# The smallest block's threshold search at an earlier priority, and four query projections requested behind the branch section

## The chip, the cores and the metric

The kernel runs on one core of a Trainium2 chip. The metric is device time in microseconds (us) for one execution; the lower the better. The core has a matrix engine (TensorE, "PE" in the rows, with its weight loads as "PEld"), a vector engine (VectorE, "DVE"), a scalar engine (ScalarE, "ACT"), GpSimd ("POOL") and SyncE ("SP"), which issues most of the transfers. Each engine works through its own instructions in a fixed order; between engines they wait on semaphores.

## The reference

One decoder layer on 1024 tokens of width 1024. A combined projection feeds two mixers: a spatial gating unit, and a sparse attention in which a light indexer scores all keys and each query attends only to the best 256 of those that it may see. Output projection and a feed-forward part follow.

```python
h    = rms_norm(x, g_pre_mix) * (1 + sc1) + sh1
proj = einsum('bsd,de->bse', h, w_in)
p_u, p_v, p_q, p_k, p_val, p_qi, p_ki, p_wi = split_cols(proj)
y_a  = spatial_gating(gelu(p_u), gelu(p_v), ...)
y_b  = dsa_attention(q, k, v, q_idx, k_idx, p_wi)
o    = concat(rms_norm(y_a), rms_norm(y_b)) @ w_out
x    = x + g1 * rms_norm(o)
x    = x + g2 * rms_norm(relu(h2 @ w_ff1)**2 @ w_ff2)
...
# dsa_attention, per block of 128 queries:
score  = sum_h w_idx * relu(q_idx . k_idx)      # causal
_, idx = lax.top_k(score, 256)
logits = q . k[idx] ; o = softmax(logits) @ v[idx]
```

## The kernel before

Queries are worked on in eight blocks of 128. Block b sees 128*(b+1) keys, so blocks 0 and 1 need no selection (at most 256 keys) and blocks 2 to 7 do. Block 2 is the smallest of these, with 384 keys. In the rows the state tiles of a block's search are called `self_...`; where a row keeps its number, `self_2640` belongs to block 2, `self_2642` to block 3 and `self_2644` to block 4.

`select(b)` looks for the 256th best score by halving: 15 rounds, one for each bit of a 16-bit key. In `search` (blocks 7, 5 and 2) a round is three DVE instructions that depend on each other: a count over all keys (L603), a comparison (L605) and a step of the threshold (L607). In `search_signs` (blocks 6, 4 and 3, the tuple `ON_ACT`) the count is done by ACT (L615), and DVE does two small instructions (L616, L617) that wait for it. After a search come a few closing instructions (L637 to L646).

Instructions are placed on each engine by a scheduler that takes them by priority, a lower number first, when by its own clock they can run. The table `PRI` gives each `select(b)` its priority. At 465000 stands `search_rest`: it sums over all six blocks how many of them need a further search (`more`, L650), a PE instruction of size 1x1 (L652) adds it over the partitions, and `V.tensor_copy` (L653) puts it in `rest`. Then a branch section, kept together by `tile_critical`, loads `rest` into a register and jumps over the further search when it is zero. Behind it `mask(7)` (L671 to L686) makes the mask for block 7, with which attention goes on.

Attention is worked in the order `OB` = 0, 7, 1, 6, 5, 4, 3, 2. The query projections of the first four of `OB` (`q_proj`, 24 PE matmuls on L301, L303 and L304 each) are placed ahead; the other four are requested inside `search_rest` and are made to follow the flag matmul L652 on PE. Attention of block 0 needs no threshold, so PE and DVE do it before the branch section.

Of the kernel before, what the change touches and what calls it, by code (L numbers as in the profile page):

```python
# [37 lines left out]
def trunk(ctx, tc, x, c, positions, w_ada, b_ada, g_pre_mix, w_in, g_sgu_v, w_spatial, b_spatial,  # L38
# [8 lines left out]
    def nm(s):  # L47
        uid[0] += 1
        return f"{s}_{uid[0]}"
# [13 lines left out]
    def p_mm():  # L63
        return ps.tile([P, 512], F32, tag="mm", name=nm("mm"))

    def p_tr():
        return ps.tile([P, 512], F32, tag="tr", name=nm("tr"), bufs=3)
# [4 lines left out]
    def ct(shape, dt, name):  # L72
        return cst.tile(shape, dt, tag=name, name=name)
# [5 lines left out]
    def stage(n):  # L79
        tc.cur_priority = n * 100000  # L80

    def after(ins, prev):
        if prev is not None:
            tc.add_manual_dep(ins.ins, prev.ins.name,
                              mybir.DependencyInfo(mybir.DependencyClass.NoSync, mybir.DependencyReason.DATA),
                              reason="in this order")
# [209 lines left out]
    def proj(p, j, wt, n, ks=range(KD)):  # L296
        h, t = hT[j // 4], (j % 4) * P
        first = None
        for k in ks:
            lh, ll = h[:, 0, k, t:t + P], h[:, 1, k, t:t + P]  # L300
            mm = T.matmul(p[:, :n], lh, wt[k][:, 0, :n], start=k == 0, stop=False)  # L301
            first = first or mm
            T.matmul(p[:, :n], lh, wt[k][:, 1, :n], start=False, stop=False)  # L303
            T.matmul(p[:, :n], ll, wt[k][:, 0, :n], start=False, stop=k == KD - 1)  # L304
        return first

    def rope(t, j, nh, pool):

        q = t.rearrange("p (h e) -> p h e", h=nh)[:, :, 0:16]
        a = pool.tile([P, 8, 16], F32, tag="ropea", name=nm("ra"), bufs=1)[:, :nh]  # L310
        b = pool.tile([P, 8, 16], F32, tag="ropeb", name=nm("rb"), bufs=1)[:, :nh]
        cb = CS[:, 0, j, None, :].to_broadcast([P, nh, 16])
        sb = CS[:, 1, j, None, :].to_broadcast([P, nh, 16])
        G.tensor_tensor(a, q, cb, op=OP.mult)
        G.tensor_tensor(b, q, sb, op=OP.mult)
        G.tensor_tensor(q[:, :, 0:8], a[:, :, 0:8], b[:, :, 8:16], op=OP.subtract)
        G.tensor_tensor(q[:, :, 8:16], a[:, :, 8:16], b[:, :, 0:8], op=OP.add)
# [240 lines left out]
    OB = (0, 7, 1, 6, 5, 4, 3, 2)  # L558

    def q_proj(b, behind=None):  # L560
        p = p_mm()
        after(proj(p, b, wQ, 512), behind)
        QT[b] = qp.tile([P, 512], F32, tag="q", name=nm("q"), bufs=8)
        A.activation(QT[b], p, AF.Copy)
        rope(QT[b], b, 8, qp)
# [7 lines left out]


    stage(5)
    PRI = ((7, 400000), (6, 405000), (5, 415000), (4, 445000), (3, 455000), (2, 460000))
    nth = ct([P, 8], F32, "nth")
    for k in range(8):
        G.memset(nth[:, k:k + 1], float(k + 1))
# [18 lines left out]
    def search(u, top, tf, cnt, kd, kk, step=lambda: None):  # L598

        V.memset(tf, float(1 << top))  # L600
        for k in range(top, -1, -1):
            step()
            V.tensor_scalar(spare[:, :u.shape[-1]], u, tf, None, op0=OP.is_ge, op1=OP.add, accum_out=cnt)  # L603
            step()
            V.tensor_scalar(kk, cnt, kd, float(1 << k), op0=OP.is_ge, op1=OP.mult)  # L605
            step()
            V.scalar_tensor_tensor(tf, tf, -float(1 << (k - 1) if k else 1), kk, op0=OP.add, op1=OP.add)  # L607
# [40 lines left out]
    def search_rest():  # L648

        V.tensor_scalar(more[:, :6], KDS, 8.0, None, op0=OP.is_gt, op1=OP.add, accum_out=more[:, 6:7])  # L650
        p = p_tr()
        flag = T.matmul(p[:1, :1], more[:, 6:7], ones, start=True, stop=True)  # L652
        V.tensor_copy(rest, p[:1, :1])  # L653
        for b in OB[4:]:
            q_proj(b, flag)
        with tc.tile_critical():
            r = V.value_load(rest)
            with V.If(r > 0):
                for b in range(2, NB):
                    cnt, sg, kk, tf, kq, lf, top8, kd, th, lo, hi = ST[b]  # L660
                    search(BI[:, boff[b]:boff[b] + P * (b + 1)].bitcast(U16), 15, lf, cnt, kd, kk, V.drain)
                V.drain()

    masked, lowest = [None], [None]

# [21 lines left out]

    for b, pri in PRI:
        tc.cur_priority = pri
# [141 lines left out]
    for u, (b, grp, pair) in enumerate(units):  # L831
        if u == 3:
            at = tc.cur_priority
            tc.cur_priority = 465000
            search_rest()
            mask(7)
            tc.cur_priority = at
        if u + 1 < len(units):
            logits(u + 1)
        values(u)  # L840
        if u in MASKS:
            mask(MASKS[u])
        if u == 12:
            u_stack.close()
            sc_stack.close()
            o_stack, op_ = push("op")
        stack_for(u + 3)
        if u % 4 == 2:
            finish_a(b)
        if u in (24, 28):  # L850
            ada_use(u // 4 - 4)
        if u in (20, 24, 28):
            ADA[u // 4 - 3] = ada_sum(u // 4 - 3)
        if u % 4 == 0 and u:
            finish(OB[u // 4 - 1])
        if u == 14:
            WO[0] = w_chunk(w_out, [(0, 0, 512)], gout, tile_of=wo_tile)
        if u >= 19 and u % 2:
            oproj0(OB[(u - 19) // 2])
# [434 lines left out]
```

## Time and profile before

| | |
|---|---|
| median of 3 runs (lowest to highest) | 1246.16 us (1245.63 to 1246.74) |
| the profiled execution's own time | 1248.28 us |
| its span in the trace | 1246.4 us |
| PE, DVE, ACT, POOL busy (share of the span) | 1164.5 (93%), 873.8 (70%), 671.2 (54%), 209.4 us (17%) |
| mean granted TensorE clock | 0.967 of full speed |

The span is the trace's time from the first to the last instruction; 1.9 us of the profiled execution's time lie around it. Busy shares are averages over all stages, and matmuls that are in flight count as busy, so PE's share does not say that PE is the bound at each place.

### The profile page before, as it was taken

Reading aid. Unit: us, or ns where it says so; the run is one execution under the profiler, and the core shown is the slowest. Engines: PE = TensorE matmul, PEld = TensorE weight load, DVE = VectorE, ACT = ScalarE, POOL = GpSimd, SP = SyncE. Lnnn points to the kernel's source line nnn. Section 1 sums busy time; section 2 is a strip of 40 time slices with the busy share of each in tenths; the row PEclk is TensorE's granted clock in tenths of the full one; section 3 lists DMA queues with packets and bytes.
Section 4 is the critical chain, followed back from the end, with each engine's and each line's share of the span. In section 5 each row is a group of like instructions: output and inputs, shape, how many; then the busy total and the mean of one; then the engine's idle time right before and its main releaser. Section 6 shows DMA issues by size and latency. Waiting matters only on the chain.

```text
span 1246.4 us, 16883 instructions
## 1 busy us (share of the span) xinstructions
PE 1164.5 (93%) x5785; PEld 985.0 (79%) x5785; DVE 873.8 (70%) x1798; ACT 671.2 (54%) x1410; POOL 209.4 (17%) x304
## 2 busy tenths in 40 slices
PE   4899989995898999899899999999999999999997
PEld 4887768884697999887687788888887888888886
DVE  7844998968478666627898775655558756876568
ACT  4554679773266755537735455555544454445452
POOL 3585605451100000012610000000000000000001
PEclk9899989996898999999999999999999999999999
DMA  9431102110000144446315753544458455533335
GB/s 343 150 93 35 52 1 64 52 64 9 1 10 29 57 161 161 172 149 215 115 60 195 269 178 127 169 143 145 161 217 331 125 188 179 197 91 99 102 98 205
DMA packets 80239, 162.41 MB, mean 130 GB/s; under 512 B 7724, under 2 KB 32920, under 8 KB 80152
## 3 DMA queue, kind: packets, MB, share of 16 engines
q1 hardware_dynamic: 80136, 161.33, 38.3%
q8 instruction: 45, 0.74, 0.3%
q14 instruction: 42, 0.34, 0.1%
q10 hardware_dynamic: 16, 0.00, 0.0%
HBM read 119.36 MB, written 41.94 MB: 129 GB/s over the span
## 4 chain that ended last, share of the span: by engine, by line
PE 51%; DVE 12%; issue 4%; DMA 3%; ACT 2%; POOL 1%; SPq 0%; DVEq 0%; POOLq 0%; ACTq 0%
PE tr L1174 8%; PE lg L1174 8%; PE mm L1174 5%; PE mm L755 4%; PE lg L991 2%; PE lg L993 2%; PE lg L992 2%; PE tr L769 2%; PE lg L730 2%; PE tr L991 2%; PE tr L993 2%; PE tr L992 2%; DVE w L882 2%; PE mm L991 1%; PE mm L993 1%
## 5 line engine op out<-in xcount | busy, mean ns | idle before, releaser
L881 ACT ACTIVATE w<-rx 128x512 fp32r<-128x512 f32 x112 | 70.7, 632 | 148.1 <-PE lg L1174 64.5
L1174 PE MATMUL tr<-w,w 128*128 128x512 f32 x504 | 134.3, 392 | 2.9 <-DVE w L882 2.9
L1174 PE MATMUL lg<-w,w 128*128 128x512 f32 x504 | 133.7, 390 | 0.0
L882 DVE TENSOR_TENSOR w<-rx,w 128x512 fp32r<-128x512 f32 x112 | 77.2, 689 | 57.8 <-ACT w L881 57.1
L301 PE MATMUL mm<-w,hT 128*128 128x512 f32 (+1 forms) x288 | 112.8, 393 | 4.7 <-ACT hT L293 3.5
L1174 PEld LDWEIGHTS tr<-w,w 128*128 128x128 f32 x504 | 95.4, 189 | 23.2 <-DVE w L882 3.4
L303 PE MATMUL mm<-w,hT 128*128 128x512 f32 (+1 forms) x288 | 111.2, 387 | 0.0
L304 PE MATMUL mm<-w,hT 128*128 128x512 f32 (+1 forms) x288 | 110.2, 384 | 1.0 <-POOL hT L294 1.0
L1174 PEld LDWEIGHTS lg<-w,w 128*128 128x128 f32 x504 | 94.9, 188 | 19.7
L1210 POOL TENSOR_TENSOR rsf<-rsf,mhalf 128x1 f32<-128x1 f32 x8 | 6.0, 752 | 605.6 <-DVE rsf L1209 605.6
L1174 PE MATMUL mm<-w,w 128*128 128x512 f32 x336 | 93.9, 389 | 0.0
L755 PEld LDWEIGHTS mm<-VV,pT 128*128 128x128 f32 x576 | 76.1, 199 | 3.8 <-ACT pT L750 1.6
L755 PE MATMUL mm<-VV,pT 128*128 128x64 f32 x576 | 76.4, 277 | 0.9 <-ACT pT L750 0.9
L1174 PEld LDWEIGHTS mm<-w,w 128*128 128x128 f32 x336 | 63.1, 188 | 13.2
L882 DVE TENSOR_TENSOR w<-b,w 128x512 fp32r<-128x512 f32 x96 | 65.7, 685 | 4.0 <-ACT w L881 4.0
L301 PEld LDWEIGHTS mm<-w,hT 128*128 128x128 f32 x288 | 55.8, 194 | 14.9 <-ACT hT L293 3.7
L730 PE MATMUL lg<-KS,qs 128*128 128x512 f32 (+5 forms) x192 | 55.3, 399 | 10.6 <-DVE mxs L731 6.0
L882 DVE TENSOR_TENSOR w<-s,w 128x512 fp32r<-128x512 f32 x56 | 38.2, 688 | 37.3 <-ACT w L881 37.3
L304 PEld LDWEIGHTS mm<-w,hT 128*128 128x128 f32 x288 | 55.0, 191 | 10.5 <-POOL hT L294 1.3
L734 ACT ACTIVATE L<-L,mxs 128x128 f32<-128x128 f32 (+7 forms) x64 | 49.2, 771 | 25.8 <-DVE mxs L731 25.6
L881 ACT ACTIVATE w<-b 128x512 fp32r<-128x512 f32 x96 | 59.4, 618 | 6.7 <-DMA b<-in_w_ff_dram 6.5
L303 PEld LDWEIGHTS mm<-w,hT 128*128 128x128 f32 x288 | 55.5, 193 | 8.5
(356 smaller groups left out, 2975.5 us busy)
## 6 DMA issues: line engine op xcount, KB each, us to landing
rx<-x_scratch SPq DMA_DIRECT2D x56, 512.0 KB, 3.5
x_scratch<-d SPq DMA_DIRECT2D x108, 256.0 KB, 3.0
ada<-in_w_ada_dram SPq DMA_DIRECT2D x48, 512.0 KB, 5.6
raw<-in_w_ff_dram SPq DMA_DIRECT2D x32, 512.0 KB, 4.1
b<-in_w_ff_dram SPq DMA_DIRECT2D x32, 512.0 KB, 4.6
x<-in_x_dram SPq DMA_DIRECT2D x16, 512.0 KB, 5.6
raw<-in_w_in_dram SPq DMA_DIRECT2D x8, 512.0 KB, 3.6
raw<-in_w_in_dram SPq DMA_DIRECT2D x16, 256.0 KB, 2.8
```

Of the source, the lines that this page charges most:

```text
L301: mm = T.matmul(p[:, :n], lh, wt[k][:, 0, :n], start=k == 0, stop=False)
L303: T.matmul(p[:, :n], lh, wt[k][:, 1, :n], start=False, stop=False)
L304: T.matmul(p[:, :n], ll, wt[k][:, 0, :n], start=False, stop=k == KD - 1)
L730: T.matmul(pl, QS[b, grp][:, q, h4 * P:(h4 + 1) * P], KS[:, grp, c0:c0 + cw], start=q == 0, stop=q == 1)
L734: ex = A.activation(L, L, AF.Exp, scale=-1.0, bias=top, accum_out=sms[:, b, h:h + 1])
L755: mm = T.matmul(po[:, o:o + 64], e[:, (si * 2 + h2) * P:(si * 2 + h2 + 1) * P], VV[:, s0 + si, grp], start=first, stop=pair == 1 and s0 + ...
L881: A.activation(hi, src, AF.Copy)
L882: eng.tensor_tensor(lo, src, hi.bitcast(F32), op=OP.subtract)
L991: ms.append(T.matmul(p, a[:, 0, k], b[:, 0, k], start=start and k == 0, stop=False, skip_group_check=more))
L992: ms.append(T.matmul(p, a[:, 0, k], b[:, 1, k], start=False, stop=False, skip_group_check=more))
L993: ms.append(T.matmul(p, a[:, 1, k], b[:, 0, k], start=False, stop=stop and k == 3, skip_group_check=more))
L1174: ms.append(T.matmul(p, x[:, qa, t * P:(t + 1) * P], y[:, qb], start=start and n == 0, stop=stop and n == 2, skip_group_check=more))
```

## The change

Two edits. Block 2's `select` is moved in `PRI` from 460000 (behind block 3) to 445000 (the number of block 4, ahead of block 3's 455000). And the loop that requests the four late query projections stands in `search_rest` behind the branch section in place of ahead of it.

```diff
-    PRI = ((7, 400000), (6, 405000), (5, 415000), (4, 445000), (3, 455000), (2, 460000))
+    PRI = ((7, 400000), (6, 405000), (5, 415000), (4, 445000), (2, 445000), (3, 455000))
...
         V.tensor_copy(rest, p[:1, :1])
-        for b in OB[4:]:
-            q_proj(b, flag)
         with tc.tile_critical():
             r = V.value_load(rest)
             with V.If(r > 0):
                 for b in range(2, NB):
                     cnt, sg, kk, tf, kq, lf, top8, kd, th, lo, hi = ST[b]
                     search(BI[:, boff[b]:boff[b] + P * (b + 1)].bitcast(U16), 15, lf, cnt, kd, kk, V.drain)
                 V.drain()
+        for b in OB[4:]:
+            q_proj(b, flag)
```

On DVE, in the stretch where block 3 searches on ACT: rows of block 2's search (`self_2640`, 384 keys) now stand between those of block 3's (`self_2642`). `ya` belongs to the gating unit.

```order
+L605 TENSOR_SCALAR self_2640<-self_2640,kds 128x1
 L616 TENSOR_SCALAR self_2642<-self_2642 128x1
+L607 SCALAR_TENSOR_TENSOR self_2640<-self_2640 128x1
 L617 SCALAR_TENSOR_TENSOR self_2642<-self_2642 128x1
+L603 TENSOR_SCALAR spare,self_2640<-BI,self_2640 128x384
+L540 SCALAR_TENSOR_TENSOR ya_2553<-tr_2552,cols,uv_2436 128x128 x2
+L605 TENSOR_SCALAR self_2640<-self_2640,kds 128x1
 L616 TENSOR_SCALAR self_2642<-self_2642 128x1
+L607 SCALAR_TENSOR_TENSOR self_2640<-self_2640 128x1
 L617 SCALAR_TENSOR_TENSOR self_2642<-self_2642 128x1
```

All 15 rounds of block 2 now stand so, about one to each of block 3's rounds; before, they stood behind block 3's last round, among the rows of block 0's attention and after them.

On DVE ahead of the branch section, before (with the semaphores that an instruction waits for):

```order
L650 TENSOR_SCALAR more<-kds 128x6
L644 MAX self_2640<-BI 128x8 [waits DVE_49]
L653 CAST rest<-tr_3131 1x1 [waits PE_49]
L646 ISA pick,self_2640<-pick,self_2640 128x8 [waits DVE_49]
L646 ISA self_2640 128x1
L656 NO_OP [waits DVE_49,Activation_49,Pool_49]
L1290 UNCONDITIONAL_BRANCH [waits DMAHW2_49,DMAHW1_49,DMAHW3_49,DMAHW0_49,DMAHW4_49,DVE_sequencer_49,DMAHW5_49,DVE_49,DMAHW6_49,PE_49,DMAHW7_49,Activation_49,Pool_49]
```

And in the change:

```order
L779 RECIPROCAL sms<-sms 128x4 [waits Activation_49]
L780 TENSOR_TENSOR yb_3083<-mm_3056,sms 128x256 [waits DVE_49,PE_49]
L795 TENSOR_SCALAR ya_3116<-ya_3116,rsa 128x512 [waits DMAHW2_49,Pool_49]
L653 CAST rest<-tr_3131 1x1 [waits PE_49]
L654 NO_OP [waits DVE_49,Activation_49,Pool_49]
L1290 UNCONDITIONAL_BRANCH [waits DMAHW2_49,DMAHW1_49,DMAHW3_49,DMAHW0_49,DMAHW4_49,DVE_sequencer_49,DMAHW5_49,DVE_49,DMAHW6_49,PE_49,DMAHW7_49,Activation_49,Pool_49]
```

The sum `more` now stands ahead of block 0's attention on DVE, so the flag follows that attention directly; the branch waits for the same engines as before, PE among them.

On PE at the place where DVE's branch section begins, before (`mm_3134` is the first late query projection):

```order
L301 MATMUL mm_3134<-w_2472,hT_143 128x512
L303 MATMUL mm_3134<-w_2472,hT_143 128x512
L1290 UNCONDITIONAL_BRANCH
L304 MATMUL mm_3134<-w_2472,hT_143 128x512
L301 MATMUL mm_3134<-w_2475,hT_143 128x512
L303 MATMUL mm_3134<-w_2475,hT_143 128x512
L304 MATMUL mm_3134<-w_2475,hT_143 128x512
```

And in the change (the same projection is `mm_3725`):

```order
L301 MATMUL mm_3725<-w_2472,hT_143 128x512
L303 MATMUL mm_3725<-w_2472,hT_143 128x512
L1290 UNCONDITIONAL_BRANCH
L304 MATMUL mm_3725<-w_2472,hT_143 128x512
L301 MATMUL mm_3725<-w_2475,hT_143 128x512
L303 MATMUL mm_3725<-w_2475,hT_143 128x512
L304 MATMUL mm_3725<-w_2475,hT_143 128x512
L709 MATMUL tr_3123<-ident,ya_3116 128x128 x3
```

In both, 20 of the projection's 24 matmuls stand between L652 and this point. Three of the four transposes of block 0's `ya` (L709), which stood ahead of L652, now stand behind the projection; and the four transposes of the second query stack of block 0 (L322), which stood behind the first logits that read the stack's low part, now stand ahead of them. SP's order is the same.

## Rows read from the trace of the kernel before

**Rows 1.** The page's chain of work that ended last, by engine

```profile
PE 51%; DVE 12%; issue 4%; DMA 3%; ACT 2%; POOL 1%; SPq 0%; DVEq 0%; POOLq 0%; ACTq 0%
```

**Rows 2.** PE's waits, 283 to 346 us: total, times, longest

```profile
PE tr L652 <- DVE more L650: 9.5, 1, 9.5
PE lg L730 <- DVE mxs L731: 5.2, 1, 5.2
```

**Rows 3.** PE's timeline, 283 to 345: start, duration, instruction, idle before and releaser

```profile
288.54 0.90 PE L730 MATMUL lg<-KS,qs 128*128 128x128 f32 x3 [3.66 <-DVE qs L392]
289.24 1.07 PE L322 MATMUL tr<-ident,qd 128*128 128x128 f32 x4
...
299.63 1.00 PE L709 MATMUL tr<-ident,ya 128*128 128x128 f32 x4
310.12 0.19 PE L652 MATMUL tr<-ones,more 128*1 128x1 f32 x2 [9.48 <-DVE more L650]
...
316.47 0.39 PE L303 MATMUL mm<-w,hT 128*128 128x512 f32 x1
...
329.43 1.22 PE L730 MATMUL lg<-KS,qs 128*128 128x512 f32 x2 [5.24 <-DVE mxs L731]
```

**Rows 4.** DVE's timeline near 300 us: one round of block 2

```profile
299.56 0.61 DVE L603 TENSOR_SCALAR_CACHE_REDUCE spare<-BI,self 128x384 int8<-128x384 int16 x1
...
300.21 0.21 DVE L605 TENSOR_SCALAR self<-self,kds 128x1 f32<-128x1 f32 x1
300.46 0.16 DVE L607 SCALAR_TENSOR_TENSOR self<-self 128x1 f32<-128x1 f32 x1
```

**Rows 5.** Line L603, 285 to 309: count, ns min/median/max, first and last start

```profile
L603 DVE TENSOR_SCALAR_CACHE_REDUCE spare<-BI,self x15: 601/612/614, 285.6 to 307.3; 128x384 int8<-128x384 int16 x15
```

**Rows 6.** Timeline of all engines, 267 to 271: rounds of block 3

```profile
267.42 0.21 DVE L616 TENSOR_SCALAR self<-self 128x1 f32<-128x1 f32 x1 [0.71 <-ACT spare L615]
...
267.67 0.16 DVE L617 SCALAR_TENSOR_TENSOR self<-self 128x1 f32<-128x1 f32 x1
...
267.92 0.72 ACT L615 ACTIVATE spare<-BI,self 128x512 int8<-128x512 int16 x1 [0.53 <-DVE self L617]
...
268.77 0.21 DVE L616 TENSOR_SCALAR self<-self 128x1 f32<-128x1 f32 x1 [0.95 <-ACT spare L615]
...
270.46 0.61 DVE L540 SCALAR_TENSOR_TENSOR ya<-tr,cols,uv 128x128 f32<-128x128 f32 x2
```

**Rows 7.** DVE's timeline near 246: blocks 5 and 4 search side by side

```profile
246.00 1.01 DVE L603 TENSOR_SCALAR_CACHE_REDUCE spare<-BI,self 128x768 int8<-128x768 int16 x1
...
247.51 1.01 DVE L603 TENSOR_SCALAR_CACHE_REDUCE spare<-BI,self 128x768 int8<-128x768 int16 x1
```

**Rows 8.** Busy time by stretch: length, then each engine, clock, DMA

```profile
258.12:265.14 7.02, 7.02 (x35) 5.88 (x34) 6.64 (x21) 3.21 (x9) 6.42 (x7) 1.00 0.22 75
265.14:283.33 18.19, 18.02 (x86) 14.89 (x84) 7.25 (x36) 13.92 (x42) 7.90 (x19) 1.00 0.21 66
283.33:300.63 17.30, 12.77 (x55) 10.97 (x53) 14.81 (x65) 7.87 (x24) 3.45 (x8) 0.61 0.00 0
```

**Rows 9.** Timeline of all engines near 263

```profile
262.89 1.29 POOL L222 TENSOR_TENSOR w<-raw,w 128x512 fp32r<-128x512 f32 x1
...
263.34 0.85 DVE L617 SCALAR_TENSOR_TENSOR self<-self 128x1 f32<-128x1 f32 x1
```

**Rows 10.** Line L617, 265 to 283.5: count, ns min/median/max

```profile
L617 DVE SCALAR_TENSOR_TENSOR self<-self x13: 159/160/286, 265.4 to 283.0; 128x1 f32<-128x1 f32 x13
```

**Rows 11.** The branch's line, 300 to 330: DVE's queue waits, ns min/median/max

```profile
L1290 DVEq EVENT_SEMAPHORE  x6: 50/50/5610, 310.9 to 317.0; - x6
```

**Rows 12.** DVE's timeline around the branch section

```profile
310.36 0.13 DVE L653 CAST rest<-tr 1x1 int32<-1x1 f32 x1
...
321.01 0.15 DVE L671 CAST seli<-self 128x1 int32<-128x1 f32 x1 [10.36 <-DVEq L656]
```

**Rows 13.** PE's waits, 345 to 640, the largest: total, times, longest

```profile
PE tr L904 <- ACT x L947: 6.2, 1, 6.2
```

## The prediction

> **What bounds the kernel now.** I began with the chain of work that ended last: half of it is PE and an eighth DVE [rows 1], so a change on DVE is worth what PE waits for it. Next I read PE's own waits in the stretch that the two edits touch. There are two of size: 9.5 us until `more` (L650) is there, so that the flag matmul can run, and 5.2 us later for DVE's `mxs` [rows 2]. PE's timeline shows where they lie. PE begins block 0's attention proper at 288.54, ends it with the transposes of `ya` at 300.63 (299.63 + 1.00), stands still until L652 at 310.12, and after the query projections stands again until 329.43 [rows 3].
>
> DVE's rows name what PE waits for at 300 to 310: rounds of block 2's search, one after the other, each a chain of L603, L605, L607 [rows 4]. All 15 begin between 285.6 and 307.3 [rows 5], behind block 3's search. Yet while block 3 searched, DVE was mostly idle. A round of block 3 is 1.35 us long (267.42 to 268.77), ACT counts through most of it, and DVE waits 0.95 us of it [rows 6]; over 265.14 to 283.33 DVE is busy for 7.25 of 18.19 us [rows 8].
>
> The second wait is a sequel of the first. After the flag's copy at 310.36 DVE stands at the branch section until L671 at 321.01 [rows 12], 5.61 us of it in one semaphore wait that ends at 317.0 [rows 11]. That is just behind the end of the 20th matmul of the first late projection (316.47 + 0.39 = 316.86 [rows 3]), the last one ahead of the branch's place on PE. Then `mask(7)` runs, and only after it can PE go on. So everything from L652 to 329.43 hangs on L652 and should move with it.
>
> **Edit 1, block 2's priority.** No work is removed: 15 rounds of 0.61 + 0.21 + 0.16 = 0.98 us move from the exposed place into block 3's search. What it takes away is PE's 9.48 us for `more` [rows 3], because the rows of the change have `more` ahead of block 0's attention. What it costs is a later end of block 3's search, and with it a later start of that attention. I work this out in four pieces.
>
> - A plain round costs nothing. L603, its accumulator read and L605 occupy DVE from 299.56 to 300.42 (300.21 + 0.21) [rows 4], 0.86 us, and the gap is 0.95 [rows 6]. L607 fits between L616 and L617, which start 0.25 apart because the second waits for the first. If this cover were too small, the rounds would stretch. The nearest row from above is blocks 5 and 4 side by side: 1.51 us for a round with twice the keys (246.00 to 247.51) [rows 7]. At that rate 14 rounds would cost 14 x (1.51 - 1.35) = 2.2. I take 0, since 384 keys need 0.4 us less than 768 (0.61 against 1.01).
> - At the start, 258.12 to 265.14, there is no gap: DVE is busy 6.64 of 7.02 us [rows 8], with block 4's closing instructions. The change puts one whole round here. I take 1.0 (0.98, rounded); bounds 0 and two rounds, 2.0.
> - Two rounds also hold a `ya` pair of 0.61 us [rows 6]. 0.86 + 0.61 is 1.47 against 0.95, so at most 0.5 each. I take 0.6 for both; bounds 0 and 1.0.
> - POOL works more in this stretch than where the rounds stood: 6.42 of 7.02 and 7.90 of 18.19 us, against 3.45 of 17.30 [rows 8]. One L617 took 0.85 us under a POOL operation that ran from 262.89 to 264.18 [rows 9], where its median is 0.16 [rows 10]. I take one such hold, 0.7; bounds 0 and two, 1.4.
>
> The Trainium skill, page "SBUF — State Buffer", section "Who interferes with whom", says why: a DVE instruction with two SBUF inputs contends with a GpSimd instruction that reads SBUF, and the one that starts second is blocked until the other ends. By that rule L607 may be held wherever POOL reads. The trace agrees at 263.34 with 0.69 us, but only there.
>
> Together the start of block 0's attention is 2.3 us later, with bounds 0 and 2.2 + 2.0 + 1.0 + 1.4 = 6.6. The closing instructions of block 2 now come ahead of that attention too, but in their place two rounds of block 2 that stood there are gone; I set these equal.
>
> **The two small moves on PE.** Three of the four `ya` transposes leave the place ahead of L652: 0.75 of 1.00 us [rows 3]. Four query-stack transposes, 0.7 us from 289.24 to the next start, go ahead of 288.54, where PE is idle for 3.66 us anyway [rows 3]. That is 1.45 us less between the start of the attention and L652; if PE waits for DVE there rather than for itself, it is 0. What could be gained beyond it: DVE now answers block 0's logits with no search rounds in between. PE is dense in that stretch, at a granted clock of 0.61 [rows 8], so I count nothing. Should the clock be full there, about 10.6 us of work would shrink by 10.6 x 0.39 = 4.1; that is the bound on the other side.
>
> **Edit 2, the projections behind the branch section.** I cost it at nothing. The built order still has the same 20 matmuls between L652 and the branch's place, and DVE's branch still names PE among the engines that it waits for. SP's order is unchanged, so no transfer moves against another; the four late projections run in the same places and are still waited on by ACT's copies and POOL's rotary steps in the same order.
>
> **The sum.** L652 comes 9.48 + 1.45 - 2.3 = 8.6 us earlier, so does the branch, `mask(7)` (L671 at 312.4 in place of 321.01) and PE's resumption (320.8 in place of 329.43). Behind that the orders differ only in neighbouring rows, and PE's waits there, the largest 6.2 us for ACT [rows 13], are for work that hangs on the same chain and moves too. The profiled execution would take 1248.28 - 8.6 = 1239.7. The median of the runs lies 2.12 us below the profiled one, so 1246.16 - 8.6 = 1237.5 us.
>
> **The rivals.**
> - *Rounds add instead of overlapping* (slower). If a round of block 3 became as long as its own 1.35 plus block 2's 0.98, block 3 would end 14 x 0.98 = 13.7 us later in place of 2.3. Then 9.48 + 1.45 - 13.7 = -2.8, and 1249.0. It decides from 10.9 / 14 = 0.78 us per round. For it: the engine runs its instructions in order, and a late L605 delays L616. Against it: 1.51 us for blocks 5 and 4 together [rows 7], although their DVE part alone is longer than block 2's.
> - *POOL holds most of the moved steps.* If all 15 L607 were held for 0.69 us, 10.4 in place of 0.7, the gain would be 8.6 - 9.7 = -1.1, and 1247.3. Against it: of 13 L617 between 265 and 283.5 the longest took 0.286 us [rows 10]. The Trainium skill's rule above, carried to its end, is this case.
> - *The lead is lost later.* If some engine behind 329 us were already bound by something that does not move, PE would wait there instead: 1246.2. For it, PE has waits up to 6.2 us later on; against it, their releasers are ACT and DVE, not transfers [rows 13].
> - *Edit 2 does free the branch*, so that DVE no longer waits for the projection: 5.6 us more [rows 11], 1231.9. Against it: the order above. The rival that edit 2 does nothing is my forecast.
>
> **How the numbers follow.** The forecast has 0.80, the rounds that add 0.06, the holds 0.04, the lost lead 0.05, the freed branch 0.05. Gains run from 9.48 + 1.45 - 6.6 = 4.3 (1241.9) to 9.48 + 1.45 + 4.1 = 15.0 (1231.1) if every cost were nothing and the clock full; that corner needs two things together, so I stop at 1231.5, which takes in the freed branch. Range 1231.5 to 1242. Within 0.2% (2.5 us, about what a measurement of this kernel can tell from no change) fall the holds and the lost lead, 0.09; slower 0.06; faster 0.85.
>
> **What would show it.** Right: L652 without a wait for `more`; L603 rows of 384 keys from about 260 to 285, one to each L616; rounds of block 3 still near 1.35 us; block 0's attention beginning on PE near 290.8; the long semaphore wait at the branch still there, near 5 to 6 us. Wrong: rounds of 2 us or more, L607 of 0.5 us and over in numbers, a new wait of PE ahead of block 0's attention of more than 10 us, or a branch section that no longer waits.

## The result, and the profile after

The changed kernel takes 1232.14 us (median of 6 runs, 1230.24 to 1233.56); the kernel before, on the same chip, took 1246.05 us (6 runs, 1239.45 to 1246.74). The ratio is 0.9896, with a 95% interval from 0.9875 to 0.9918: 13.9 us faster. The forecast was 1237.5 us, so the sign and the range held, and the gain was 5.3 us larger than worked out. The profiled execution took 1231.81 us, its span 1229.8 us, and the mean granted clock was 0.977 (0.967 before).

The first lines of the page of the changed kernel (busy time by engine; the chain that ended last):

```profile
PE 1156.0 (94%) x5785; PEld 977.9 (80%) x5785; DVE 869.4 (71%) x1798; ACT 671.2 (55%) x1410; POOL 208.6 (17%) x304
...
PE 57%; DVE 10%; DMA 3%; issue 2%; ACT 2%; POOL 1%; SPq 0%; DVEq 0%; POOLq 0%; ACTq 0%
```

PE, DVE, ACT and POOL are busy for nearly as long as before; the chain has 57% of PE where it had 51% [rows 1]. PE's waits from 283 to 346 us in the changed kernel (total, times, longest):

```profile
PE lg L730 <- DVE mxs L731: 4.8, 1, 4.8
...
```

The 9.5 us for `more` [rows 2] are gone; the wait for `mxs` is still there, 0.4 us shorter. PE's timeline of the changed kernel:

```profile
289.69 1.83 PE L730 MATMUL lg<-KS,qs 128*128 128x128 f32 x6 [4.25 <-DVE qs L392]
...
298.37 0.19 PE L652 MATMUL tr<-ones,more 128*1 128x1 f32 x2
298.49 0.50 PE L301 MATMUL mm<-w,hT 128*128 128x512 f32 x1
...
315.88 3.10 PE L730 MATMUL lg<-KS,qs 128*128 128x512 f32 x6 [4.80 <-DVE mxs L731]
```

Block 0's attention begins at 289.69 (288.54 before, [rows 3]), L652 runs at 298.37 with nothing to wait for (310.12), and PE goes on behind `mask(7)` at 315.88 (329.43). All 15 rounds of block 2 now lie beside block 3's search. Lines L603 and L607 of the changed kernel, 258 to 290 (count, ns min/median/max, first and last start):

```profile
L603 DVE TENSOR_SCALAR_CACHE_REDUCE spare<-BI,self x15: 600/605/613, 260.4 to 283.8; 128x384 int8<-128x384 int16 x15
L607 DVE SCALAR_TENSOR_TENSOR self<-self x15: 146/149/434, 264.9 to 284.7; 128x1 f32<-128x1 f32 x15
```

And how a round of each fits into the other, in the timeline of all engines of the changed kernel:

```profile
268.87 0.21 DVE L616 TENSOR_SCALAR self<-self 128x1 f32<-128x1 f32 x1
...
269.20 0.60 DVE L603 TENSOR_SCALAR_CACHE_REDUCE spare<-BI,self 128x384 int8<-128x384 int16 x1
...
269.37 0.72 ACT L615 ACTIVATE spare<-BI,self 128x512 int8<-128x512 int16 x1
...
269.85 0.21 DVE L605 TENSOR_SCALAR self<-self,kds 128x1 f32<-128x1 f32 x1
...
270.22 0.21 DVE L616 TENSOR_SCALAR self<-self 128x1 f32<-128x1 f32 x1 [0.16 <-ACT spare L615]
```

This round of block 3 is still 1.35 us long (268.87 to 270.22), and DVE, after a whole round of block 2 inside it, still waits 0.16 us for ACT. By stretch (length, then PE, PEld, DVE, ACT and POOL busy, clock, DMA):

```profile
258.12:265.14 7.02, 7.02 (x35) 5.88 (x34) 6.99 (x21) 3.26 (x12) 6.80 (x10) 1.00 0.27 75
265.14:284.35 19.21, 17.77 (x84) 14.47 (x82) 17.49 (x95) 14.95 (x41) 7.53 (x19) 1.00 0.21 63
...
289.69:298.37 8.68, 8.65 (x42) 7.82 (x43) 4.99 (x26) 5.03 (x20) 0.61 (x1) 0.64 0.00 0
```

In the second stretch DVE was busy for 7.25 us before [rows 8] and for 17.49 us now; the stretch is 1.0 us longer. The last line is block 0's attention up to L652: 8.68 us, where it was 12.09 (288.54 to 300.63) [rows 3]. The branch's wait on DVE, and the first instruction behind it:

```profile
L1290 DVEq EVENT_SEMAPHORE  x6: 50/50/3985, 299.0 to 303.4; - x6
```
```profile
307.47 0.15 DVE L671 CAST seli<-self 128x1 int32<-128x1 f32 x1 [8.72 <-DVEq L654]
```

The wait is 3.99 us, 1.6 less than in [rows 11]. The clock that was granted to PE, in the changed kernel:

```profile
289.69:294.00 4.31, 4.28 (x20) 0.50 0.00 0
...
296.00:298.37 2.37, 2.37 (x15) 1.00 0.00 0
298.37:303.50 5.13, 5.13 (x25) 1.00 0.00 0
```

and in the kernel before:

```profile
288.54:298.50 9.96, 9.82 (x43) 0.50 0.00 0
298.50:300.63 2.13, 2.13 (x8) 0.54 0.02 4
...
310.12:314.00 3.88, 3.88 (x11) 0.50 0.00 0
314.00:317.00 3.00, 3.00 (x15) 0.98 0.00 0
```

Both kernels begin block 0's attention at the lower level (1.2 GHz). In the kernel before PE stays at it nearly to the end of that attention, stands still for 9.48 us and begins the late projection at it again; in the changed kernel PE is at 2.4 GHz from about 296 on.

### The profile page after: what moved, and what is told of

It is laid out like the page before. It is cut to its first block, busy times and chain, and to the rows that moved or that the text cites. A ratio compares the mean times of both kernels' runs of the same rounds, so it can differ in the third digit from the quotient of the medians.

```text
span 1229.8 us, 16884 instructions
## 1 busy us (share of the span) xinstructions
PE 1156.0 (94%) x5785; PEld 977.9 (80%) x5785; DVE 869.4 (71%) x1798; ACT 671.2 (55%) x1410; POOL 208.6 (17%) x304
## 4 chain that ended last, share of the span: by engine, by line
PE 57%; DVE 10%; DMA 3%; issue 2%; ACT 2%; POOL 1%; SPq 0%; DVEq 0%; POOLq 0%; ACTq 0%
PE tr L1174 8%; PE lg L1174 8%; PE mm L1174 6%; PE mm L755 4%; PE lg L991 3%; PE lg L993 3%; PE lg L992 3%; PE tr L991 2%; PE tr L993 2%; PE tr L992 2%; PE mm L993 2%; PE mm L992 2%; PE mm L991 2%; PE tr L769 2%; PE lg L730 2%
## 5 line engine op out<-in xcount | busy, mean ns | idle before, releaser
L304 PEld LDWEIGHTS mm<-w,hT 128*128 128x128 f32 x288 | 54.7, 190 | 10.2 <-POOL hT L294 1.0
L730 PE MATMUL lg<-KS,qs 128*128 128x512 f32 (+5 forms) x192 | 52.2, 384 | 10.7 <-DVE mxs L731 5.7
```

What stands on the lines that cost most here:

```text
L730: T.matmul(pl, QS[b, grp][:, q, h4 * P:(h4 + 1) * P], KS[:, grp, c0:c0 + cw], start=q == 0, stop=q == 1)
```

## The experiments

Starting times in different traces are compared as they stand. The traces of before and of the change are in step to 0.04 us ahead of block 2's rounds (L638 of block 4 at 259.02 and 259.06), but those of the other runs reach that place up to 1.6 us earlier or 0.6 later. Where that matters, the text counts from a nearer place.

The theory was that the moved search is nearly the whole gain, that edit 2 does nothing, and that the 5.3 us beyond the forecast come from a shorter stretch of block 0 and from the clock at the projection. Rivals were that edit 2 frees the branch, that the cover in block 3's search is not what made the move cheap, and that the shorter stretch comes from PE's clock or from DVE alone.

### Edit 1 alone

The kernel before with the new `PRI` line and nothing else.

```diff
-    PRI = ((7, 400000), (6, 405000), (5, 415000), (4, 445000), (3, 455000), (2, 460000))
+    PRI = ((7, 400000), (6, 405000), (5, 415000), (4, 445000), (2, 445000), (3, 455000))
```

> Edit 1 alone; the four projections stay requested ahead of the branch section. Theory (the whole gain is edit 1, edit 2 changes no engine's order): the changed kernel's time, 1232 us within 2, and a DVE wait at the branch of about 4 us as there. Rival (edit 2 frees part of the branch wait): slower than the changed kernel by 1.5 to 5 us.

Measured: 1232.89 us (1231.61 to 1236.97), ratio 0.991 [0.9885, 0.9935]. L652 runs at 298.38 and PE goes on at 315.96. Within the spread, edit 1 is the whole gain. One thing differs from the changed kernel: this execution begins block 0's attention 0.7 us earlier (288.98) and needs 9.40 us up to L652 in place of 8.68, with the same 42 matmuls in the same order. What that shows of the clock is taken up further down.

### Edit 2 alone

The kernel before with the second edit and nothing else.

```diff
-        for b in OB[4:]:
-            q_proj(b, flag)
         with tc.tile_critical():
...
                 V.drain()
+        for b in OB[4:]:
+            q_proj(b, flag)
```

> Edit 2 alone; block 2's search stays behind block 3's. Theory: no change from the kernel before, 1246 us within 2.5, with PE's 9.5 us wait for the sum and DVE's 5.6 us wait at the branch as there. Rival: 2 to 6 us faster, with a shorter wait at the branch.

Measured: 1244.51 us (1239.77 to 1248.03), ratio 0.9992 [0.9975, 1.001]: no change. PE's waits, 283 to 346, and DVE's branch line:

```profile
PE tr L652 <- DVE more L650: 9.9, 1, 9.9
PE lg L730 <- DVE mxs L731: 5.2, 1, 5.2
```
```profile
L1290 DVEq EVENT_SEMAPHORE  x6: 49/50/5250, 309.6 to 315.3; - x6
```

Both waits of PE are there as in the kernel before, and the branch's wait, 5.25 us, is near its 5.61. Requesting the projections behind the section does not move them behind it, as the built order showed.

### The branch truly freed

The changed kernel; the late projections follow the first DVE instruction of `mask(7)` in place of the flag matmul, so that all 24 matmuls of the first one stand behind the branch's place on PE (`opened[0]` is that first instruction).

```diff
-        for b in OB[4:]:
-            q_proj(b, flag)
...
             mask(7)
+            for b_ in OB[4:]:
+                q_proj(b_, opened[0])
```

> The changed kernel, but the projections are requested behind the mask of block 7 and made to follow its first DVE instruction in the scheduler's order, so that none of their matmuls stands ahead of the branch on PE; no wait between engines is added. Theory (DVE's wait at the branch is for the 20 matmuls of the first projection): that wait falls from 4.0 us to under 1, the mask of block 7 starts 3 to 4 us earlier, PE resumes 3 to 4 us earlier, and the time is 1228 to 1229.5 us. Rival (the section is held by its own load and fetch, or PE loses elsewhere what DVE gains): 1231 to 1233.

Measured: 1226.69 us (1221.6 to 1230.18), ratio 0.9861 [0.9836, 0.9885], a larger gain than the 1228 to 1229.5 us expected. It is the lowest median so far; its interval and that of edit 1 alone, from the same runs of before, only touch, at 0.9885, and it overlaps that of the changed kernel by 0.001. DVE's branch line, and PE's first logits behind `mask(7)`:

```profile
L1291 DVEq EVENT_SEMAPHORE  x6: 49/50/353, 298.1 to 298.9; - x6
```
```profile
322.31 1.53 PE L729 MATMUL lg<-KS,qs 128*128 128x512 f32 x6
```

The wait fell from 3.99 to 0.35 us, `mask(7)` begins at 302.92 in place of 307.47 (5.47 us behind the flag, and 9.10 in the changed kernel), and PE meets no wait for `mxs` there (4.80 us in the changed kernel). All 96 matmuls of the four late projections now stand ahead of those logits; in the changed kernel 48 do, and the logits behind the other 48 begin at 330.69.

### The idle stretch ahead of block 0's attention filled

The changed kernel with 18 matmuls added on PE (their result is not used) in the 4.25 us wait ahead of block 0's attention. For that the second query stack (`stack_for(2)`) is requested ahead of them in place of behind the first logits.

```diff
     stack_for(0)
+    at = tc.cur_priority
+    tc.cur_priority = 465000
+    stack_for(2)
+    tc.cur_priority = at
+    pf = p_mm()
+    for i in range(18):
+        T.matmul(pf, hT[0][:, 0, i % KD, :P], wQ[i % KD][:, 0], start=True, stop=True)
     logits(0)
-    stack_for(2)
```

> The changed kernel with 18 extra 128x512 matmuls (4.1 us at full clock) into an unused tile on PE, in the 4.3 us that it idles ahead of block 0's attention; their result is not read. Theory (the lower granted clock after that idle time costs time in block 0's attention, 289.7 to 298.4): the clock stays at full there, the stretch of 8.7 us shrinks by 1.5 to 3, and the time falls by as much, 1229 to 1231 us. Rival (the stretch is bound by the hand-overs between PE, DVE and ACT, so that the clock does not matter): 8.7 us still, and 1232 us or a little more for the extra work.

Measured: 1229.84 us (1225.79 to 1229.95), ratio 0.9865 [0.9839, 0.989]. PE's wait fell to 0.94 us, yet the granted clock of its stretches was:

```profile
288.35:290.00 1.65, 1.05 (x6) 1.00 0.00 0
290.00:292.00 2.00, 1.94 (x12) 0.75 0.00 0
292.00:294.00 2.00, 2.00 (x13) 0.50 0.00 0
```

The clock fell all the same, inside the stretch in place of ahead of it, and the stretch up to L652 took 8.40 us in place of 8.68. The time lies in the range that was expected for a clock that stays up, but not for that reason. From L618, the end of block 3's search, to L652 it is 13.54 us (283.21 to 296.75) where the changed kernel takes 14.02 (284.35 to 298.37): 0.5 us of the 2.3 by the medians. No row here accounts for the rest. So this run does not tell what a full clock all through would be worth.

### Block 2's count done twice

The changed kernel, in which each round of block 2 does its L603 a second time (added work, the same threshold).

```diff
             V.tensor_scalar(spare[:, :u.shape[-1]], u, tf, None, op0=OP.is_ge, op1=OP.add, accum_out=cnt)
+            if twice:
+                V.tensor_scalar(spare[:, :u.shape[-1]], u, tf, None, op0=OP.is_ge, op1=OP.add, accum_out=cnt)
...
-            search(u, 14, tf, cnt, kd, kk)
+            search(u, 14, tf, cnt, kd, kk, twice=b == 2)
```

> The changed kernel, but each of block 2's 15 rounds makes its count twice (0.6 us more on DVE per round; the second count gives the same number). Theory (a round is hidden because its 0.86 us fit in DVE's 0.95 us gap, and hardly more fits): rounds of block 3 stretch from 1.35 to about 1.9 us, block 3's search ends 7 to 8 us later, and the time is 1238 to 1241 us. Rival (DVE has room, the cover is much larger than a round): under 3 us later, 1232 to 1235.

Measured: 1242.34 us (1240.25 to 1249.0), ratio 0.9974 [0.9954, 0.9994]. One of block 3's rounds (L616 is L618 here) in DVE's timeline, from its start to the next:

```profile
273.15 0.21 DVE L618 TENSOR_SCALAR self<-self 128x1 f32<-128x1 f32 x1
275.09 0.21 DVE L618 TENSOR_SCALAR self<-self 128x1 f32<-128x1 f32 x1
```

The one shown takes 1.94 us in place of 1.35, and the twelve from 265.42 to 287.33 take 1.83 on average (1.34 to 2.27). PE waits 2.8 us for `more` again. So the gap of 0.95 us that ACT's count leaves on DVE is the cover, and a round that is larger than it does stretch block 3. The size was not met. Counted from L638 (L640 here, at 258.12), block 3's search ends 6.6 us later than in the changed kernel (7 to 8 expected), the flag runs 5.9 and `mask(7)` begins 7.5 us later, and 10.2 of the 13.9 us are lost, more than expected. What is lost behind `mask(7)` no row here shows.

### Block 0's attention with DVE loaded

The changed kernel with 8 counts over 384 keys (4.9 us of DVE's time in the trace) added on DVE among block 0's logits, where the kernel before had its search rounds; the counts go to a tile of their own.

```diff
+                if b == 0:
+                    V.tensor_scalar(spare[:, :384], BI[:, boff[2]:boff[3]].bitcast(I16), 0.0, None, op0=OP.is_ge,
+                                    op1=OP.add, accum_out=load)
```

> The changed kernel with eight extra counts of 384 keys (0.69 us each with their accumulator read, 5.5 us in all, result not read) on DVE among the logits of block 0's attention, where seven rounds of block 2 stood in the kernel before. Theory (that stretch became shorter mainly because PE's work is dense enough to get its full clock back by 294.9; a DVE that answers later thins PE's work and keeps the clock low): the stretch grows from 8.7 to 10.5 us or more, the clock is at half through most of it, and the first late projection starts at the half clock; 1234.5 to 1238 us. Rival (DVE's answers are hidden, PE's own work sets the stretch): 8.7 to 9.3 us, and 1232 to 1233 us.

Measured: 1234.4 us (1231.01 to 1235.63), ratio 0.990 [0.9878, 0.9922]. The granted clock of PE's stretches:

```profile
294.00:297.00 3.00, 2.97 (x15) 0.50 0.00 0
297.00:299.72 2.72, 2.72 (x15) 0.92 0.00 0
```

The stretch is 9.84 us long, 1.16 more than in the changed kernel and 2.25 less than before. It falls between the two expectations. All of the 1.16 us lies ahead of the first long logits (128x512): from the start to them it is 7.03 us (289.88 to 296.91) where the changed kernel takes 5.84 (289.69 to 295.53). So a loaded DVE can hold up this stretch in the new order. The last part, with the full clock, is there with or without the load (2.81 and 2.84 us).

### PE's wait for the flag filled, in part

The kernel before with 28 added matmuls ahead of the flag matmul, into a tile that the flag overwrites.

```diff
         p = p_tr()
+        for i in range(28):
+            T.matmul(p, hT[0][:, 0, i % KD, :P], wQ[i % KD][:, 0], start=True, stop=True)
         flag = T.matmul(p[:1, :1], more[:, 6:7], ones, start=True, stop=True)
```

> The kernel before, with 28 added 128x512 matmuls on PE between the transposes of block 0's ya and the flag matmul, into a tile that the flag matmul overwrites afterwards, so that PE works through most of its 9.48 us wait for more. Nothing else is moved but the last transposes and values of block 0, which now stand ahead of the flag. The clock theory (about 1.7 us of the change's gain is the first late projection at the full clock, because PE no longer stands still ahead of it): the granted clock at the projection is 1.00 in place of 0.50, DVE's long wait at the branch falls from 5.6 to about 4.0 us, mask(7) begins 1.6 us earlier behind the flag, and the time falls by 1 to 2 us, 1244 to 1245. The rival (the branch wait fell for another reason, such as what stands ahead of it on DVE, and the projection's clock does not matter): the wait stays at 5.3 us or more and the time is that of the kernel before, within 1 us. If the fill itself runs past DVE's last round, the flag is late, and L652 will show a wait for nothing but PE.

Measured: 1246.51 us (1242.94 to 1249.45), ratio 1.0003 [0.9988, 1.0018]. PE's timeline at the flag (L654 here), and DVE's branch line:

```profile
298.62 6.76 PE L653 MATMUL tr<-w,hT 128*128 128x512 f32 x28
...
312.44 0.19 PE L654 MATMUL tr<-ones,more 128*1 128x1 f32 x2 [4.94 <-DVE more L650]
312.56 0.79 PE L301 MATMUL mm<-w,hT 128*128 128x512 f32 x1
```
```profile
L1292 DVEq EVENT_SEMAPHORE  x6: 49/50/5301, 313.3 to 319.1; - x6
```

By the numbers the rival won, but PE had 4.94 us of idle time left, and the projection began at 0.79 and 0.63 us a matmul, as before. The flag came 2.3 us later than before (3.4 counted from the start of block 0's attention, which is at 287.45 here), since the last values of block 0 were now behind the fill and DVE waited 2.5 us for them. PE's order behind the flag changed too: all 96 matmuls of the late projections stand ahead of the next logits, where the kernel before has 48. So this run alone left the theory untested, and its time is no price of the clock.

### The same, filled up to the flag

46 added matmuls in place of 28.

```diff
-        for i in range(28):
+        for i in range(46):
```

> As the filled wait above, with 46 added matmuls in place of 28, so that PE has work up to the flag (the 28 left it idle for 4.94 us, and seven matmuls of the first late projection then still took 0.63 us). The clock theory: with under 0.5 us of idle time ahead of the flag, at most one matmul of the first late projection takes 0.63 us, DVE's long wait at the branch is near 4.0 us in place of 5.3, and mask(7) begins 9.1 us behind the flag matmul in place of 10.65 in the run with 28. The rival (the wait at the branch is longer in the kernels with the old priorities for another reason): it stays at 5.2 us or more. The time moves by no more than 1.5 us either way, since the flag itself may be some tenths late.

Measured: 1250.0 us (1245.38 to 1252.64), ratio 1.0037 [1.0017, 1.0057]. PE's wait is 1.23 us, and:

```profile
313.02 0.19 PE L654 MATMUL tr<-ones,more 128*1 128x1 f32 x2 [1.23 <-DVE more L650]
...
313.14 0.50 PE L301 MATMUL mm<-w,hT 128*128 128x512 f32 x1
```
```profile
L1292 DVEq EVENT_SEMAPHORE  x6: 49/50/3997, 313.9 to 318.3; - x6
```

With the old priorities and a busy PE the projection runs at the full clock and the branch's wait is 4.00 us, as in the changed kernel. `mask(7)` begins 9.58 us behind the flag matmul (10.65 with 28; 9.1 was expected). The time rose nonetheless, by more than the 1.5 us expected: the flag is 2.9 us later than before (3.2 counted from the start of block 0's attention, at 288.22), and PE's order changed again (72 matmuls ahead of the next logits), with waits of 1.5 us for `mxs` and 2.5 us for ACT's copy of a projection. So the branch's wait is what the two filled runs show; their times mix it with the fill's costs.

### The branch freed with the old priorities

The edit of the freed branch on the old `PRI` line (against that run):

```diff
-    PRI = ((7, 400000), (6, 405000), (5, 415000), (4, 445000), (2, 445000), (3, 455000))
+    PRI = ((7, 400000), (6, 405000), (5, 415000), (4, 445000), (3, 455000), (2, 460000))
```

> The kernel before with its priorities, and the four late projections made to follow the first DVE instruction of mask(7), so that all 24 matmuls of the first one stand behind the branch's place on PE. If the wait at the branch is set by the projection alone, it falls from 5.6 to under 1 us here too, mask(7) begins near 315.5 in place of 321.0, PE resumes 3 to 5 us earlier, and the time is 1241 to 1243. PE's wait for more stays near 9.5 us. The rival (behind the branch some other work takes the place of the projection, or the projections, being later, delay PE by as much as the branch gains): the wait falls but the time stays within 1 us of 1246.

Measured: 1248.75 us (1244.46 to 1251.09), ratio 1.0021 [1.0006, 1.0035]: 2.4 us slower by the medians. The branch's wait falls to 0.53 us and PE goes on 5.5 us earlier (4.8 counted from the flag, at 309.43 here), as expected, but:

```profile
323.90 1.22 PE L729 MATMUL lg<-KS,qs 128*128 128x512 f32 x2 [6.10 <-DVE mxs L730]
```

Here only 24 of the 96 projection matmuls stand ahead of these logits, 72 behind (48 and 48 before). PE waits 6.1 us with nothing to do, and then does what the kernel before did inside the wait, the first 4 us (323.9 to 328) at a granted clock of 0.50. The rival named it, though for 1246 within 1 us: the later projections take what the branch gave, and more. The next long logits begin at 343.56, only 1.3 us ahead of before (0.7 counted from the flag), and by the last of them (523.3 against 522.3) that is gone too.

### The projections ahead, the branch not freed

The changed kernel, in which block 7's last first-pair logits and the transposes of its first probabilities follow all four projections, so that 96 matmuls stand ahead as in the freed branch (`asked[0]` is the last matmul of the last late projection).

```diff
+                    if u == 4 and h2 == 1 and i == 1 and q == 0:
+                        after(mm, asked[0])
...
+                if u == 4:
+                    after(tr, asked[0])
```

> The changed kernel, in which the last logits of block 7's first pair and its first transposes of probabilities are made to follow all four late projections, so that 96 matmuls stand ahead of them on PE as in the run with the freed branch (48 in the changed kernel); the branch still waits for the first projection. If the freed branch gained by the order on PE alone (work that needs no mask fills the wait for it), the time is the same as there, 1226 to 1228. If it gained by the earlier branch, PE meets a wait of about 5 us here as well, for the value that DVE takes from the second matmul tile only after mask(7) (0.6 us there), and the time is that of the changed kernel, 1231 to 1233. The wait at the branch stays near 4.0 us by both.

Measured: 1237.1 us (1233.81 to 1241.2), ratio 0.9929 [0.9909, 0.9949], some 5 us slower than the changed kernel. PE's wait:

```profile
320.99 0.79 PE L303 MATMUL mm<-w,hT 128*128 128x512 f32 x1 [8.48 <-ACT q L566]
```

It is longer than the 5 us expected and for another releaser: the third projection needs the copy of the second on ACT, which stands behind ACT's exponentials of block 7, and these wait 11.88 us for DVE's `mxs` behind `mask(7)`. So the order on PE alone does not make the freed branch's gain; without the earlier mask the fill runs into that wait. How much of that gain each of the two is worth where both are there, no run separates.

## Why the prediction was right in sign and small in size

**Removed wait.** Right. 9.48 us for `more` are gone, and edit 1 alone removes them.

**Plain rounds cost nothing.** Right: 1.35 us before and after, with 0.16 us of DVE's wait left, and a doubled count makes the rounds 1.83 us on average.

**The delay of block 0's attention, 2.3 us.** Mis-sized: 1.15 us (289.69 against 288.54), and the pieces are others than those priced. Block 3's rounds start with L616 and its search ends with L618, which before ran at 283.33. In the changed kernel:

```profile
266.07 0.20 DVE L616 TENSOR_SCALAR self<-self 128x1 f32<-128x1 f32 x1
...
267.52 0.21 DVE L616 TENSOR_SCALAR self<-self 128x1 f32<-128x1 f32 x1
...
283.36 0.21 DVE L616 TENSOR_SCALAR self<-self 128x1 f32<-128x1 f32 x1 [0.16 <-ACT spare L615]
...
283.82 0.60 DVE L603 TENSOR_SCALAR_CACHE_REDUCE spare<-BI,self 128x384 int8<-128x384 int16 x1
...
284.35 0.14 DVE L618 TENSOR_SCALAR self<-self 128x1 f32<-128x1 f32 x1
```

The whole round at the start (1.0) puts off one L616 by 0.93 us (265.14 before), but by the next only 0.10 are left (267.42 before, [rows 6]), for DVE had waited there for ACT. The two rounds with a `ya` pair (0.6) put off the next L616 by 0.26 and 0.15 us, most of which the round behind makes up. The later rounds bring the delay to 0.59 us at the last L616 (282.77 before), and the last count of block 2, which stands ahead of L618, adds 0.43. So the search ends 1.02 us later, and that this equals the round that was put at its start is luck. From L618 to PE's start it is 5.34 us, and was 5.21; that the closing instructions add next to nothing was right.

The hold by POOL (0.7) comes once, behind L618:

```profile
284.67 0.46 POOL L314 TENSOR_TENSOR ra<-q,CS 128x128 f32<-128x128 f32 x1
284.71 0.43 DVE L607 SCALAR_TENSOR_TENSOR self<-self 128x1 f32<-128x1 f32 x1
```

It cost 0.29 us (0.434 - 0.149), and L607 ends with POOL's instruction. The Trainium skill's rule on a two-input DVE instruction beside a GpSimd read ("SBUF — State Buffer", "Who interferes with whom") agrees with this row. What kept the other L607 short is that they seldom meet such a read: in the timeline 11 of the 15 begin while POOL runs nothing. The prediction's reading that the trace of before shows a hold only at 263.34 was wrong: L641 there took 1.92 us from 260.45, beside POOL's L222, and over the same 640 keys 0.89 in the changed kernel.

**The stretch of block 0, 1.45 us shorter.** Mis-sized: 12.09 - 8.68 = 3.41. The moved transposes are worth what was priced, 0.76 us for L709 and 0.73 for L322. The term put all else at nothing, and it is 1.92 us. The last long logits and values, before:

```profile
296.50 1.63 PE L730 MATMUL lg<-KS,qs 128*128 128x512 f32 x3
297.93 0.95 PE L755 MATMUL mm<-VV,pT 128*128 128x64 f32 x4
298.63 1.20 PE L730 MATMUL lg<-KS,qs 128*128 128x512 f32 x2
```

and in the changed kernel:

```profile
295.53 1.13 PE L730 MATMUL lg<-KS,qs 128*128 128x512 f32 x3
296.50 1.00 PE L755 MATMUL mm<-VV,pT 128*128 128x64 f32 x8
297.30 0.94 PE L730 MATMUL lg<-KS,qs 128*128 128x512 f32 x3
```

From start to next start, three long logits took 1.43 us before and take 0.83 at 297.30. All six took 3.00 and take 1.80, and the twelve matmuls of the values took 2.27 and take 1.65: together 1.82 of the 1.92 us. So it is the clock, 1.00 from 296.00 on in the changed kernel and 0.50 to 0.54 before. The run of edit 1 alone bears it out with the same matmuls in the same order: 5.83 us up to the first long logits, as in the changed kernel (5.84), and then 3.57 us in place of 2.84, at a clock of 0.50 up to 296.3 and 0.67 in the next us. Why the level rises earlier in one kernel or execution than in another, no run shows. DVE's quicker answers do not appear as a gain of their own: the short logits (128x128) took 3.00 us before and take 3.21. They are a condition, for with DVE loaded PE loses 1.2 us ahead of the long logits. The prediction's bound for the clock was itself too small: the 0.61 that it used is of the longer stretch from 283.33, and block 0's attention alone ran at 0.51, which gives 10.6 x 0.49 = 5.2 in place of 4.1.

**L652.** By these terms 9.48 + 3.41 - 1.15 = 11.7 us earlier, and the rows say 310.12 - 298.37 = 11.75 (forecast 8.6).

**The branch section moves as it is.** Not quite: it moved and also shrank, and the sign of a wait near 5 to 6 us did not hold. From L652 to L671 it took 10.89 us and now takes 9.10, since the wait for the first late projection went from 5.61 to 3.99. In the prediction the clock's bound was for block 0's attention alone. That PE stood still ahead of the projection, and that the first nine of its matmuls took 0.53 to 0.79 us where the later ones took 0.39, stood in the trace of before and was put at nothing. The runs settle it: the wait is 3.96 to 4.02 us where PE was busy up to the flag or nearly so (the change, edit 1 alone, the idle stretch filled, DVE loaded, the projections ahead, the full fill on the old priorities), and 5.19 to 5.61 us where it had stood still for 9.48, 9.9, 2.83 and 4.94 us (before, edit 2 alone, the doubled count, 28 matmuls). The two filled runs differ only in the number of added matmuls, and in the one with 28 PE had been at the full clock ahead of its wait (28 matmuls in 6.76 us), so there the standing still alone brought it down. 11.75 + 1.8 = 13.5, which is the 13.55 us by which PE resumes earlier, and the medians' 13.9 within their spread. Beside the forecast, 1.15 us are from the smaller delay, 1.96 from the stretch of block 0 and 1.8 from the branch section.

**Edit 2 costs nothing and frees nothing.** Right, by edit 2 alone.

**Rivals.** Rounds that add: no. POOL's holds: no, one of 0.29 us. The lead lost later: no; behind the resumption it stays (the logits behind the second pair of late projections at 344.90 before, 330.69 after; the last logits at 522.3 and 506.5). The freed branch: not by this change; made so by another edit it gives 5.5 to 6.2 us more by the medians on top of edit 1 (1226.69 against 1232.14 and 1232.89), and a loss of 2.4 on the old priorities. Its median is the lowest of all that were run, though its interval overlaps that of the filled idle stretch (0.9839 to 0.989).

## What to carry to other kernels

A chain of small dependent steps belongs beside another such chain that waits for a different engine, as long as its share of a round fits into the other's gap; read that gap from the rows, and expect the gain to end where it is filled. When a wait of PE is removed, price also the work behind it at the clock that PE then has, from the durations of the same matmuls at either level in the trace at hand. A wait that is shortened pays only if what stood inside it as cover is still ahead of it: here the same freed branch gained 5 to 6 us with 96 matmuls ahead of the next dependent instruction and lost 2.4 with 24. More matmuls ahead without the earlier branch lost 5 us, so neither pays alone. And add up the pieces of a term against the trace even when its total came out: the delay here agreed with a piece that had all but vanished by the next round.

## What the runs showed of the hardware that was not expected

From the end of the branch's semaphore wait to the first DVE instruction behind the section it takes about 4 us in every kernel: 317.0 to 321.01 before, 303.4 to 307.47 in the change, 298.9 to 302.92 with the branch freed, though the branch jumps over all that it guards. No experiment here was aimed at it.

PE's clock stayed at 0.50 through ten us of block 0's attention before, in which PE was busy for 9.82 of 9.96 us, mostly with 128x128 and 128x64 matmuls, and it fell in that work even behind 18 added matmuls. In the changed kernel and in the run of edit 1 alone, the same matmuls in the same order reached the full clock at different places, which made 0.7 us between them. At the first late projection, behind 9.48 us in which PE stood still, it was 0.50 from 310.12 to 314 and 0.98 from 314 to 317.
